# Stick-breaking attention: value product by query tiles on the two halves of the array, issued for two steps together

## The chip, the cores and the metric

The kernel runs on one core of one Trainium2 chip. The metric is the device time of one execution in microseconds (us). Each number of the trace comes from one profiled execution. In the text, PE is TensorE, DVE is VectorE, ACT is ScalarE, POOL is GpSimd, SP is the engine that issues the transfers.

## The reference

One residual block over 2048 tokens of width 1024 in float32: an RMSNorm, one wide input projection, a state-space branch (SSD), a stick-breaking attention branch of 16 heads of size 64, gates, an output projection and a second RMSNorm. The change touches the attention branch alone, cut here to what matters:

```python
def stick_breaking(q, k, v):
    for blk in range(L // SB_BLOCK):                       # 128 queries
        logits = einsum('bqhd,bkhd->bhqk', q[:, q0:kend], k[:, :kend]) * scale
        mask = ki < qi
        log_fail = where(mask, log_sigmoid(-logits), 0.0)
        between = cumsum(log_fail, axis=3, reverse=True) - log_fail
        w = where(mask, exp(log_sigmoid(logits) + between), 0.0)
        outs.append(einsum('bhqk,bkhd->bqhd', w, v[:, :kend]))
...
y_sb = einsum('ble,ed->bld', o * silu(z_sb), w_sb_proj)
```

## The kernel before

Products that need full precision (the projections, `proj` in the trace) are written as three products of rounded float32 pieces: high by high, high by low, low by high (`product`, L139). Each is a matmul of 128 rows, 128 columns and 512 moving columns. All matmuls and transposes are chained in program order (`chain`, L68), so the order on PE is the order in the code. The other engines' orders are set by a planner from the program, the priorities and the buffers.

The attention works on **steps** `(h, qs, kc)` (L778): a head, a block of 512 queries, a block of 512 keys with `kc <= qs`, taken from the diagonal `kc == qs` down to 0. A head has ten steps: four on the diagonal, six off it; there are 160 steps. A step has four query tiles `i` of 128 queries:

- `attn_qk(s, i)` (L826): two matmuls give the logits `lg` (PSUM, two buffers); ACT makes two sigmoids, `tc` (L840) and `sw` (L842). POOL masks both on the diagonal; DVE runs the product scan over `tc` (L849) and multiplies it into `sw` (L850). POOL keeps the carry for the next key block (L853).
- `attn_tr(s, i)` (L859): PE transposes the 128x128 pieces of `sw` into `wtp` (PSUM, three buffers), ACT copies them to `wt` (L870), which collects the weights of the whole step, keys on partitions, for the four key pieces `kb`.
- `attn_av(s)` (L872): the value product. For each of the four `kb`, the stationary operand is `v[:, kb, :]` (128 keys by 64 columns) and the moving one `wt[:, kb, :]`. Even `kb` write partitions 0 to 63 of `po`, odd `kb` 64 to 127, so that two of them can run on the two halves of the array's columns. On the diagonal, `kb` 2 and 3 leave out the queries ahead of them, `kb` 1 doesn't: POOL sets that corner of `wt` to zero (L869).
- After the last step of a query block (`kc == 0`): ACT copies one half of `po` (L889), DVE adds the other (L890) and multiplies by the gate `zl` (L891), which a transfer brought (L887). The result leaves to `otd` (L892).

The step loop (L902 to L910) runs `attn_tr(s, i)`, then `attn_qk(s + 1, i)`, then `fill(i)`: some projection matmuls that are not part of the attention, given out evenly over the steps (`fill`, L787; 24 of them make one tile of a projection). After `i == 1` comes `attn_av(s - 1)` and one more filling, `fill(CPB)`. In the last head the filling comes from the next stage (`fill_y`, L765), which needs a norm across tokens first (`first_y`, L737). Then follow the output projections (from L917), which read `otd`.

Of the kernel before, what the change touches and what calls it, by code (L numbers as in the profile page):

```python
# [9 lines left out]
F32 = mybir.dt.float32  # L10
# [8 lines left out]
P = 128  # L19
D = 1024  # L20
KT = D // P
TB = 512
HEADS = 16
HD = 64
# [24 lines left out]
def hybrid_kernel(ctx, tc, x, norm_pre, w_in, b_gate, conv_w, conv_b, dt_bias, a_log, d_skip,  # L49
                  ssd_norm, w_ssd_proj, w_sb_proj, w_out, norm_post, out, dbg=None):  # L50
    nc = tc.nc
# [3 lines left out]
    CPB = TB // P  # L55
# [12 lines left out]
    def chain(i):  # L68
        if last_pe[0] is not None:
            after(i, last_pe[0])  # L70
        last_pe[0] = i

    def matmul(*a, **k):
        chain(nc.tensor.matmul(*a, **k))  # L74

    def transpose(*a):
        chain(nc.tensor.transpose(*a))  # L77

    def opened(*a, **k):
        cm = tc.tile_pool(*a, **k)  # L80
        return cm.__enter__(), lambda: cm.__exit__(None, None, None)
# [31 lines left out]
    otd = [drp.tile([D, TB], F32, name=f"otd{t}") for t in range(NTB)]  # L113
    zsd = [drp.tile([D, TB], F32, name=f"zsd{t}") for t in range(NTB)]
# [94 lines left out]
    gz, close_gz = opened(name="gz", bufs=2)  # L209
# [433 lines left out]
    ab, close_ab = opened(name="ab", bufs=1)  # L643
    ap, close_ap = opened(name="ap", bufs=1, space=PSUM)
# [120 lines left out]
    def fill_y(box):  # L765
        tb, mp, y = TBO[0], box["mp"], box["y"]
        for dt in range(KT):
            w = prep_w(wa, WA, w_ssd, dt * P)
            ps = pp.tile([P, TB], F32, name="proj", tag="pp")
            yield from product(ps, w, *y)  # L770
            gt = piece("o")
            nc.sync.dma_start(gt, gtd[tb][dt * P:(dt + 1) * P, :])
            nc.vector.tensor_mul(mp[:, dt, :], gt, ps)
# [4 lines left out]
    steps = [(h, qs, kc) for h in range(HEADS) for qs in reversed(range(NTB)) for kc in reversed(range(qs + 1))]  # L778
# [3 lines left out]
    def tick():  # L782
        clock[0] += 1
        while events and events[0][0] <= clock[0]:
            heapq.heappop(events)[2]()

    def fill(i):  # L787
        f = fills
        if f["pos"] <= 0:
            for _ in f["gen"]:  # L790
                tick()
            if f["late"]:
                return
            f.update(gen=fill_y(box_y), left=8 * 24, pos=len(FW) * (len(steps) - last_head) - 3, acc=0.0, late=True)
        f["acc"] += f["left"] / f["pos"] * FW[i]
        f["pos"] -= 1
        while f["acc"] >= 1.0:
            f["acc"] -= 1.0
            f["left"] -= 1
            if next(f["gen"], 0) == 0:  # L800
                f["left"] = 0
                break
            tick()

    kts, vts, qts, pos, carry, ws = {}, {}, {}, {}, {}, {}

    def attn_load(s):
        if s >= len(steps):
            return
        h, qs, kc = steps[s]  # L810
        if (h, qs) not in qts:
            qa = ab.tile([P, TB], F32R, name="qa", tag="qa", bufs=2)
            qb = ab.tile([P, TB], F32R, name="qb", tag="qb", bufs=2)
            cols = slice(qs * TB, (qs + 1) * TB)
            nc.sync.dma_start(qa.bitcast(F32), qst[h][:, cols])
            nc.sync.dma_start(qb[0:HD].bitcast(F32), qst[h][HD:P, cols])
            nc.sync.dma_start(qb[HD:P].bitcast(F32), qst[h][0:HD, cols])
            qts[h, qs] = qa, qb
        if (h, kc) not in kts:
            k = ab.tile([P, TB], F32R, name="kt", tag="kt", bufs=4)  # L820
            nc.sync.dma_start(k.bitcast(F32), kst[h][:, kc * TB:(kc + 1) * TB])
            v = ab.tile([P, CPB, HD], F32, name="vt", tag="vt", bufs=4)
            nc.sync.dma_start(v, vst[h // 4][:, h % 4, kc * CPB:(kc + 1) * CPB, :])
            kts[h, kc], vts[h, kc] = k, v

    def attn_qk(s, i):  # L826
        if s >= len(steps):
            return
        h, qs, kc = steps[s]
        diag = kc == qs  # L830
        W = (i + 1) * P if diag else TB
        qa, qb = qts[h, qs]
        k = kts[h, kc]
        qc = slice(i * P, (i + 1) * P)
        lg = ap.tile([P, TB], F32, name="lg", tag="lg", bufs=2)
        matmul(lg[:, :W], qa[:, qc], k[:, :W], start=True, stop=False)
        matmul(lg[:, :W], qb[:, qc], k[:, :W], start=False, stop=True)
        t = ab.tile([P, TB + 1], F32, name="tc", tag="tc", bufs=5)
        nc.gpsimd.memset(t[:, W:W + 1], 1.0)  # L839
        nc.scalar.activation(t[:, :W], lg[:, :W], AF.Sigmoid, scale=-0.125)  # L840
        w = ab.tile([P, TB], F32, name="sw", tag="sw", bufs=6)
        nc.scalar.activation(w[:, :W], lg[:, :W], AF.Sigmoid, scale=0.125)  # L842
        if diag:
            nc.gpsimd.affine_select(out=t[:, W - P:W], in_=t[:, W - P:W], compare_op=ALU.is_gt, fill=1.0, base=0,  # L844
                                    pattern=[[-1, P]], channel_multiplier=1)
            nc.gpsimd.affine_select(out=w[:, W - P:W], in_=w[:, W - P:W], compare_op=ALU.is_gt, fill=0.0, base=0,
                                    pattern=[[-1, P]], channel_multiplier=1)
        tr = t[:, W::-1]
        nc.vector.tensor_tensor_scan(tr, tr, tr, 1.0 if diag else carry[h, qs, i], ALU.mult, ALU.min)  # L849
        nc.vector.tensor_mul(w[:, :W], w[:, :W], t[:, 1:W + 1])  # L850
        if kc > 0:
            c = ab.tile([P, 1], F32, name="cy", tag="cy", bufs=8)
            nc.gpsimd.tensor_copy(c, t[:, 0:1])  # L853
            carry[h, qs, i] = c
        ws[s, i] = w

    wts = {}

    def attn_tr(s, i):  # L859
        h, qs, kc = steps[s]  # L860
        n = i + 1 if kc == qs else CPB
        tp = ap.tile([P, TB], F32, name="wtp", tag="wtp", bufs=3)
        sw = ws.pop((s, i))
        for kb in range(n):
            transpose(tp[:, kb * P:(kb + 1) * P], sw[:, kb * P:(kb + 1) * P], ident)
        if i == 0:
            wts[s] = ab.tile([P, CPB, TB], F32, name="wt", tag="wt", bufs=2)
            if kc == qs:
                nc.gpsimd.memset(wts[s][:, 1, 0:P], 0.0)  # L869
        nc.scalar.copy(wts[s][:, 0:n, i * P:(i + 1) * P], tp[:, 0:n * P].rearrange("p (k q) -> p k q", q=P))  # L870

    def attn_av(s):  # L872
        h, qs, kc = steps[s]
        if (h, qs) not in pos:
            pos[h, qs] = ap.tile([P, TB], F32, name="po", tag="po", bufs=1)
        po, v = pos[h, qs], vts[h, kc]
        wt = wts.pop(s)
        for kb in range(CPB):
            lo = kb * P if kc == qs and kb > 1 else 0
            e = (kb % 2) * HD  # L880
            matmul(po[e:e + HD, lo:], v[:, kb, :], wt[:, kb, lo:], start=(kc == qs and kb < 2),
                   stop=(kc == 0 and kb >= 2), skip_group_check=True)
        if kc == 0:
            e0 = (h % 2) * HD
            mine, other = slice(e0, e0 + HD), slice(HD - e0, P - e0)
            z = ab.tile([P, TB], F32, name="zl", tag="zl", bufs=1)
            nc.sync.dma_start(z[mine], zsd[qs][h * HD:(h + 1) * HD, :])  # L887
            o = gz.tile([P, TB], F32, name="o", tag="gz", bufs=2)
            nc.scalar.copy(o[mine], po[other])  # L889
            nc.vector.tensor_add(o[mine], o[mine], po[mine])  # L890
            nc.vector.tensor_mul(o[mine], o[mine], z[mine])  # L891
            nc.sync.dma_start(otd[qs][h * HD:(h + 1) * HD, :], o[mine])  # L892

    attn_load(0)
    attn_load(1)
    for tb in range(NTB):
        if tb == NTB - 1:
            for i in range(CPB):
                later(1 + 6 * i, lambda i=i: attn_qk(0, i))
        run(proj(wg, tb, done_g(0, tb)))  # L900
    flush()
    for s in range(len(steps)):  # L902
        attn_load(s + 2)
        for i in range(CPB):
            attn_tr(s, i)
            attn_qk(s + 1, i)
            fill(i)
            if i == 1 and s > 0:
                attn_av(s - 1)
                fill(CPB)  # L910
    attn_av(len(steps) - 1)
    for _ in fills["gen"]:
        pass
# [3 lines left out]
    with tc.tile_pool(name="fc", bufs=1) as fc, tc.tile_pool(name="fp", bufs=1, space=PSUM) as fp:  # L917
# [65 lines left out]
        for it, tb in enumerate(TBO):  # L983
# [3 lines left out]
            for dt in range(KT):  # L987
# [11 lines left out]
                po = pp.tile([P, TB], F32, name="proj", tag="pp")  # L999
# [65 lines left out]
```

## Time and profile before

| | us |
|---|---|
| time, median of 3 runs (lowest to highest) | 3057.37 (3057.05 to 3060.44) |
| time of the profiled execution | 3057.36 |
| its span, first to last instruction | 3055.6 |
| PE busy | 3012.0 (99%) |
| DVE busy | 2140.1 (70%) |
| ACT busy | 1585.5 (52%) |
| POOL busy | 505.3 (17%) |
| value product: busy PE, in 1280 records | 283.5 |
| copy of one half of the product on ACT, 64 times, median of one | 0.58 |

The value products stand between 943 and 2556 us of the span. A float32 matmul of the value product is two records in the trace; a transpose and a matmul of rounded float32 are one. Ends of matmuls are modelled and overlap with the next, so the times between the starts tell how fast PE goes, not the durations.

### The profile page before, as it was taken

The numbers are of one execution on the slowest core, as the hardware profiler recorded it, in microseconds if no ns is written. First come the engines' busy times: TensorE is split into PE (matmuls) and PEld (weight loads), VectorE is DVE, ScalarE is ACT, GpSimd is POOL, SyncE is SP. The second block draws the span as 40 slices with busy tenths as digits, with TensorE's granted clock in tenths as the row PEclk, the third lists the DMA queues.
The fourth block names the chain that finished last, engine by engine and source line by source line (L and its number), as shares of the span: only waits on it lengthen the run. The fifth ranks groups of instructions, "written<-read, shape, count | busy, mean of one in ns | idle before, by whom it ended". The sixth has DMA issues, their size and how long they took to land.

```text
span 3055.6 us, 47953 instructions
## 1 busy us (share of the span) xinstructions
PE 3012.0 (99%) x16169; PEld 2342.6 (77%) x16169; DVE 2140.1 (70%) x3653; ACT 1585.5 (52%) x3102; POOL 505.3 (17%) x1690
## 2 busy tenths in 40 slices
PE   8999999999999999999999999999999999999998
PEld 6899888788887777777777777777777667888887
DVE  7310578868877777878778878877777798756653
ACT  6221345534546666666666666666666565333321
POOL 0000001001101222222222221222122331101000
PEclk9999999999999999999999999999999999999999
DMA  5522122202233333324323333334233345545452
GB/s 166 142 72 52 28 58 77 78 25 76 81 90 109 101 86 94 93 85 108 94 77 101 97 86 96 89 90 118 66 87 92 114 136 158 178 131 179 131 165 70
DMA packets 298812, 303.84 MB, mean 99 GB/s; under 512 B 55916, under 2 KB 196040, under 8 KB 298568
## 3 DMA queue, kind: packets, MB, share of 16 engines
q1 hardware_dynamic: 298416, 300.73, 34.3%
q8 instruction: 130, 2.13, 0.3%
q14 instruction: 114, 0.93, 0.1%
q10 hardware_dynamic: 152, 0.05, 0.0%
HBM read 208.28 MB, written 92.41 MB: 98 GB/s over the span
## 4 chain that ended last, share of the span: by engine, by line
PE 88%; DVE 7%; DMA 3%; issue 1%; ACT 0%; POOL 0%; SPq 0%; ACTq 0%; DVEq 0%; POOLq 0%
PE proj L74 49%; PE po L74 14%; PE lg L74 8%; PE wtp L77 8%; PE vps L74 6%; DMA csb<-csd 3%; DVE acc L472 1%; PE yp L74 1%; DVE S L538 1%; DVE csb L520 1%; DVE dl L518 1%; DVE dl L514 1%; PE stp L74 0%; DMA xt<-in_x 0%; DVE wlo L134 0%
## 5 line engine op out<-in xcount | busy, mean ns | idle before, releaser
L74 PE MATMUL proj<-hh,whi 128*128 128x512 f32 x1920 | 765.1, 398 | 0.0
L74 PE MATMUL proj<-hl,whi 128*128 128x512 f32 x1920 | 763.0, 397 | 1.1 <-DVE hl L286 0.9
L74 PE MATMUL proj<-hh,wlo 128*128 128x512 f32 x1920 | 763.8, 398 | 0.0
L870 ACT COPY wt<-wtp 128x512 f32<-128x512 f32 (+3 forms) x640 | 336.4, 526 | 396.2 <-PE wtp L77 374.5
L849 DVE TENSOR_TENSOR_SCAN tc<-tc,cy 128x513 f32<-128x513 f32 x384 | 491.7, 1281 | 56.0 <-ACT tc L840 52.3
L850 DVE TENSOR_TENSOR sw<-sw,tc 128x512 f32<-128x512 f32 (+3 forms) x640 | 400.8, 626 | 74.6 <-POOL cy L853 1.4
L74 PEld LDWEIGHTS proj<-hh,whi 128*128 128x128 f32 x1920 | 361.9, 188 | 102.2 <-issue 31.8
L74 PEld LDWEIGHTS proj<-hl,whi 128*128 128x128 f32 x1920 | 361.7, 188 | 102.0 <-issue 31.1
L74 PEld LDWEIGHTS proj<-hh,wlo 128*128 128x128 f32 x1920 | 361.5, 188 | 100.0 <-issue 31.1
L849 DVE TENSOR_TENSOR_SCAN tc<-tc 128x129 f32<-128x129 f32 (+3 forms) x256 | 220.6, 862 | 201.2 <-POOL tc L844 200.3
L840 ACT ACTIVATE tc<-lg 128x512 f32<-128x512 f32 (+3 forms) x640 | 346.3, 541 | 14.5 <-PE lg L74 3.2
L842 ACT ACTIVATE sw<-lg 128x512 f32<-128x512 f32 (+3 forms) x640 | 344.8, 539 | 0.0
L77 PE MATMUL wtp<-ident,sw 128*128 128x128 f32 x2176 | 341.7, 272 | 0.0
L77 PEld LDWEIGHTS wtp<-ident,sw 128*128 128x128 f32 x2176 | 275.5, 140 | 80.1 <-issue 0.3
L74 PE MATMUL lg<-kt,qa 128*128 128x512 f32 (+3 forms) x640 | 284.2, 444 | 2.7 <-ACT sw L842 2.5
L74 PE MATMUL po<-wt,vt 128*64 128x512 f32 (+2 forms) x1280 | 283.5, 554 | 1.7 <-ACT wt L870 1.7
L132 ACT CAST whi<-wraw 128x512 fp32r<-128x512 f32 x248 | 154.4, 623 | 240.9 <-PE proj L74 155.2
L74 PE MATMUL lg<-kt,qb 128*128 128x512 f32 (+3 forms) x640 | 234.3, 366 | 0.0
L134 DVE TENSOR_TENSOR wlo<-wraw,whi 128x512 fp32r<-128x512 f32 x246 | 174.2, 709 | 72.7 <-ACT whi L132 70.1
L74 PEld LDWEIGHTS po<-wt,vt 128*64 128x64 f32 x1280 | 77.9, 136 | 151.9 <-issue 139.1
L504 POOL TENSOR_TENSOR xe<-xd,dec 128x512 f32<-128x512 f32 x32 | 49.8, 1556 | 829.5 <-DVE xd L502 829.5
L839 POOL MEMSET tc<- 128x1 f32 x640 | 62.6, 98 | 739.5 <-DVE sw L850 720.0
(199 smaller groups left out, 4660.1 us busy)
## 6 DMA issues: line engine op xcount, KB each, us to landing
wraw<-in_w_in SPq DMA_DIRECT2D x120, 256.0 KB, 3.0
csb<-csd SPq DMA_DIRECT2D x64, 256.0 KB, 4.3
qa<-qst SPq DMA_DIRECT2D x64, 256.0 KB, 3.7
qb<-qst SPq DMA_DIRECT2D x128, 128.0 KB, 3.8
kt<-kst SPq DMA_DIRECT2D x64, 256.0 KB, 3.3
gtd<-zb SPq DMA_DIRECT2D x64, 256.0 KB, 2.1
wraw<-in_w_ssd_proj SPq DMA_DIRECT2D x64, 256.0 KB, 3.0
scr<-gtd SPq DMA_DIRECT2D x64, 256.0 KB, 3.2
```

The source lines that it names most:

```text
L74: chain(nc.tensor.matmul(*a, **k))
L77: chain(nc.tensor.transpose(*a))
L132: nc.scalar.copy(h, raw)
L134: (eng or nc.vector).tensor_tensor(l, raw, h.bitcast(F32), op=ALU.subtract)
L472: nc.vector.scalar_tensor_tensor(acc, xp[:, i:i + TB], pv[:, col:col + 1], acc, op0=ALU.mult, op1=ALU.add)
L504: nc.gpsimd.tensor_tensor(heads(xe), heads(xd), tok(dec), op=ALU.mult)
L839: nc.gpsimd.memset(t[:, W:W + 1], 1.0)
L840: nc.scalar.activation(t[:, :W], lg[:, :W], AF.Sigmoid, scale=-0.125)
L842: nc.scalar.activation(w[:, :W], lg[:, :W], AF.Sigmoid, scale=0.125)
L849: nc.vector.tensor_tensor_scan(tr, tr, tr, 1.0 if diag else carry[h, qs, i], ALU.mult, ALU.min)
L850: nc.vector.tensor_mul(w[:, :W], w[:, :W], t[:, 1:W + 1])
L870: nc.scalar.copy(wts[s][:, 0:n, i * P:(i + 1) * P], tp[:, 0:n * P].rearrange("p (k q) -> p k q", q=P))
```

## The change

`attn_av` gives each half of the array two of the four query tiles instead of two of the four key pieces. Tiles 0 and 3 go to partitions 0 to 63, tiles 1 and 2 to partitions 64 to 127 (`GROUPS`). So each `kb` is issued twice, with the same stationary operand, over 256 moving columns; for tiles 0 and 3 they lie in two runs of 128. On the diagonal, tiles that lie ahead of the key piece are left out one by one, and the zeroed corner isn't needed. All of a query's sum then lies in one half: the copy on ACT and the addition on DVE go, and one DVE product of 128x256 with the gate takes their place. The gate comes in two transfers instead of one, the result leaves in two.

The value products of steps `s - 2` and `s - 1` are issued together, at even `s`, after `i == 1`; those of the last two steps follow the loop. `fill(CPB)` keeps its place in every step, and stands in step 0 too. Buffers: `wt` 2 to 3, `po` 1 to 2 (of half the size), `zl` 1 to 2 (half), `wtp` 3 to 2, `tc` 5 to 4, `sw` 6 to 5.

```diff
-        t = ab.tile([P, TB + 1], F32, name="tc", tag="tc", bufs=5)
+        t = ab.tile([P, TB + 1], F32, name="tc", tag="tc", bufs=4)
...
-        w = ab.tile([P, TB], F32, name="sw", tag="sw", bufs=6)
+        w = ab.tile([P, TB], F32, name="sw", tag="sw", bufs=5)
...
-        tp = ap.tile([P, TB], F32, name="wtp", tag="wtp", bufs=3)
+        tp = ap.tile([P, TB], F32, name="wtp", tag="wtp", bufs=2)
...
-            wts[s] = ab.tile([P, CPB, TB], F32, name="wt", tag="wt", bufs=2)
-            if kc == qs:
-                nc.gpsimd.memset(wts[s][:, 1, 0:P], 0.0)
+            wts[s] = ab.tile([P, CPB, TB], F32, name="wt", tag="wt", bufs=3)
...
+    GROUPS = ((0, 3), (1, 2))
...
-            pos[h, qs] = ap.tile([P, TB], F32, name="po", tag="po", bufs=1)
+            pos[h, qs] = ap.tile([P, 2, P], F32, name="po", tag="po", bufs=2)
...
         for kb in range(CPB):
-            lo = kb * P if kc == qs and kb > 1 else 0
-            e = (kb % 2) * HD
-            matmul(po[e:e + HD, lo:], v[:, kb, :], wt[:, kb, lo:], start=(kc == qs and kb < 2),
-                   stop=(kc == 0 and kb >= 2), skip_group_check=True)
+            for g, (q0, q1) in enumerate(GROUPS):
+                ts = [t for t in (q0, q1) if kc < qs or t >= kb]
+                if not ts:
+                    continue
+                j0 = (q0, q1).index(ts[0])
+                step = (q1 - q0) * P
+                src = wt[:, kb, ts[0] * P:ts[0] * P + P]
+                if len(ts) == 2:
+                    src = wt[:, kb, :].rearrange("p (t q) -> p t q", q=P)[:, q0:q1 + 1:q1 - q0, :]
+                    dst = po[g * HD:(g + 1) * HD, :, :]
+                else:
+                    dst = po[g * HD:(g + 1) * HD, j0, :]
+                matmul(dst, v[:, kb, :], src, start=(kc == qs and kb == 0),
+                       stop=(kc == 0 and kb == (CPB - 1 if kc < qs else ts[-1])), skip_group_check=True)
         if kc == 0:
...
-            nc.sync.dma_start(z[mine], zsd[qs][h * HD:(h + 1) * HD, :])
-            o = gz.tile([P, TB], F32, name="o", tag="gz", bufs=2)
-            nc.scalar.copy(o[mine], po[other])
-            nc.vector.tensor_add(o[mine], o[mine], po[mine])
-            nc.vector.tensor_mul(o[mine], o[mine], z[mine])
-            nc.sync.dma_start(otd[qs][h * HD:(h + 1) * HD, :], o[mine])
+            zr = zsd[qs][h * HD:(h + 1) * HD, :].rearrange("d (t q) -> d t q", q=P)
+            orow = otd[qs][h * HD:(h + 1) * HD, :].rearrange("d (t q) -> d t q", q=P)
+            z = ab.tile([P, 2, P], F32, name="zl", tag="zl", bufs=2)
+            for g, (q0, q1) in enumerate(GROUPS):
+                nc.sync.dma_start(z[g * HD:(g + 1) * HD], zr[:, q0:q1 + 1:q1 - q0, :])
+            nc.vector.tensor_mul(z, z, po)
+            for g, (q0, q1) in enumerate(GROUPS):
+                nc.sync.dma_start(orow[:, q0:q1 + 1:q1 - q0, :], z[g * HD:(g + 1) * HD])
...
-            if i == 1 and s > 0:
+            if i == 1 and s > 0 and s % 2 == 0:
+                attn_av(s - 2)
                 attn_av(s - 1)
+            if i == 1:
                 fill(CPB)
+    attn_av(len(steps) - 2)
     attn_av(len(steps) - 1)
```

On PE, before, at the value product of the first step, which lies on the diagonal (`hh` and `hl` are the projections' moving operands, `whi` and `wlo` their weights):

```order
L74 MATMUL proj<-hh_195,wlo 128x512
L74 MATMUL po<-wt,vt 64x512 x2
L74 MATMUL po<-wt,vt 64x256
L74 MATMUL po<-wt,vt 64x128
L74 MATMUL proj<-hh_195,whi 128x512
```

and one step further down, at the value product of the second step, off the diagonal:

```order
L74 MATMUL proj<-hh_195,wlo 128x512
L74 MATMUL proj<-hh_196,whi 128x512
L74 MATMUL po<-wt,vt 64x512 x4
L74 MATMUL proj<-hl_200,whi 128x512
L74 MATMUL proj<-hh_196,wlo 128x512
```

On PE now, at the value products of the same two steps:

```order
L74 MATMUL proj<-hh_196,whi 128x512
L74 MATMUL po<-wt,vt 64x256 x2
L74 MATMUL po<-wt,vt 64x128
L74 MATMUL po<-wt,vt 64x256
L74 MATMUL po<-wt,vt 64x128 x3
L74 MATMUL po<-wt,vt 64x256 x8
L74 MATMUL proj<-hl_200,whi 128x512
L74 MATMUL proj<-hh_196,wlo 128x512
```

The two groups of value products have become one, with projection matmuls ahead of it and behind it as before; 4 and 4 matmuls have become 7 and 8, none of more than 256 columns.

On DVE, before, at the end of the third query block of the first head (L849 is the scan, L850 the product with it):

```order
L849 SCALAR_TENSOR_TENSOR tc<-tc 128x257
L850 TENSOR_TENSOR sw<-sw,tc 128x256
L890 TENSOR_TENSOR o<-o,po 64x512
L891 TENSOR_TENSOR o<-o,zl 64x512
L849 SCALAR_TENSOR_TENSOR tc<-tc 128x385
L850 TENSOR_TENSOR sw<-sw,tc 128x384
```

and now, at the end of its third and fourth query block:

```order
L849 SCALAR_TENSOR_TENSOR tc<-tc,cy 128x513
L850 TENSOR_TENSOR sw<-sw,tc 128x512
L899 TENSOR_TENSOR zl<-zl,po 128x256 x2
L849 SCALAR_TENSOR_TENSOR tc<-tc,cy 128x513
L850 TENSOR_TENSOR sw<-sw,tc 128x512
```

Two instructions per query block have become one; where a pair of steps ends two query blocks, both stand together, one step later for the first.

## Rows read from the trace of the kernel before

**Rows 1.** The page's busy time, share and instructions of an engine.
```profile
PE 3012.0 (99%) x16169; PEld 2342.6 (77%) x16169; DVE 2140.1 (70%) x3653; ACT 1585.5 (52%) x3102; POOL 505.3 (17%) x1690
```
**Rows 2.** Stretches: length, busy of PE, PEld, DVE, ACT, POOL; clock, DMA, GB/s.
```profile
930.00:1330.00 400.00, 400.00 (x2047) 286.56 (x2046) 316.19 (x393) 260.08 (x549) 98.37 (x402) 1.00 0.35 93
...
2410.00:2510.00 100.00, 91.27 (x449) 64.36 (x448) 84.64 (x122) 64.16 (x133) 38.03 (x93) 0.93 0.45 141
2510.00:2556.00 46.00, 41.63 (x212) 28.12 (x210) 39.96 (x52) 28.96 (x64) 14.53 (x36) 1.00 0.31 91
```
**Rows 3.** Timeline, start and length: value product off the diagonal, PE and PEld.
```profile
1706.87 0.40 PE L74 MATMUL proj<-hh,whi 128*128 128x512 f32 x1
...
1707.20 1.94 PE L74 MATMUL po<-wt,vt 128*64 128x512 f32 x8
1707.68 0.14 PEld L74 LDWEIGHTS po<-wt,vt 128*64 128x64 f32 x2 [0.29 <-issue]
...
1708.11 0.14 PEld L74 LDWEIGHTS po<-wt,vt 128*64 128x64 f32 x2 [0.28 <-issue]
...
1709.07 0.50 PE L74 MATMUL proj<-hl,whi 128*128 128x512 f32 x1
...
1709.40 0.39 PE L74 MATMUL proj<-hh,wlo 128*128 128x512 f32 x1
```
**Rows 4.** Instructions of that block by 1708.05: ns min/median/max, first and last start.
```profile
L74 PE MATMUL po<-wt,vt x4: 592/618/643, 1707.2 to 1707.7; 128*64 128x512 f32 x4
```
**Rows 5.** Timeline, start and length: value product on the diagonal.
```profile
1143.15 0.39 PE L74 MATMUL proj<-hl,whi 128*128 128x512 f32 x1
...
1143.38 0.40 PE L74 MATMUL proj<-hh,wlo 128*128 128x512 f32 x1
...
1143.70 1.50 PE L74 MATMUL po<-wt,vt 128*64 128x512 f32 x8
...
1145.14 0.50 PE L74 MATMUL proj<-hh,whi 128*128 128x512 f32 x1
...
1145.47 0.40 PE L74 MATMUL proj<-hl,whi 128*128 128x512 f32 x1
```
**Rows 6.** Half-array matmuls of 128 columns (SSD), 700.0 to 701.8, as rows 4.
```profile
L74 PE MATMUL yp<-dl,xd x16: 272/273/323, 700.1 to 701.5; 128*64 128x128 f32 x16
L74 PEld LDWEIGHTS yp<-csb,S x16: 137/137/137, 700.2 to 701.6; 128*64 128x64 f32 x16
L74 PE MATMUL yp<-csb,S x16: 272/273/273, 700.3 to 701.7; 128*64 128x128 f32 x16
```
**Rows 7.** The page's group of value products: busy us, mean ns | idle before.
```profile
L74 PE MATMUL po<-wt,vt 128*64 128x512 f32 (+2 forms) x1280 | 283.5, 554 | 1.7 <-ACT wt L870 1.7
```
**Rows 8.** Timeline of one step: a tile's way from logits to transposes; copies of `wtp`.
```profile
1701.72 0.60 PE L77 MATMUL wtp<-ident,sw 128*128 128x128 f32 x4
...
1702.35 0.59 ACT L870 COPY wt<-wtp 128x512 f32<-128x512 f32 x1 [0.57 <-PE wtp L77]
...
1705.26 0.38 PE L77 MATMUL wtp<-ident,sw 128*128 128x128 f32 x2
...
1705.40 0.48 PE L74 MATMUL lg<-kt,qa 128*128 128x512 f32 x1
...
1709.40 0.69 DVE L850 TENSOR_TENSOR sw<-sw,tc 128x512 f32<-128x512 f32 x1
...
1715.48 0.60 PE L77 MATMUL wtp<-ident,sw 128*128 128x128 f32 x4
```
**Rows 9.** The same timeline: an issue on SP.
```profile
1712.69 0.59 SPq L887 DMA_DIRECT2D zl<-zsd  x1
```
**Rows 10.** Waits of SP, 940 to 2560: total, times, longest.
```profile
SPq L892 <- DVE o L891: 180.7, 60, 8.2
```
**Rows 11.** Waits of PE, 2410 to 2556, the two longest, columns as rows 10.
```profile
PE sps L74 <- DVE scr L708: 3.9, 1, 3.9
PE proj L74 <- ACT zb L203: 3.6, 1, 3.6
```

More of the change, by code (lines that the diff above doesn't have):

```diff
@@ L878, in attn_av @@
         for kb in range(CPB):
-            lo = kb * P if kc == qs and kb > 1 else 0
-            e = (kb % 2) * HD
-            matmul(po[e:e + HD, lo:], v[:, kb, :], wt[:, kb, lo:], start=(kc == qs and kb < 2),
-                   stop=(kc == 0 and kb >= 2), skip_group_check=True)
-        if kc == 0:
-            e0 = (h % 2) * HD
-            mine, other = slice(e0, e0 + HD), slice(HD - e0, P - e0)
-            z = ab.tile([P, TB], F32, name="zl", tag="zl", bufs=1)
-            nc.sync.dma_start(z[mine], zsd[qs][h * HD:(h + 1) * HD, :])
-            o = gz.tile([P, TB], F32, name="o", tag="gz", bufs=2)
-            nc.scalar.copy(o[mine], po[other])
-            nc.vector.tensor_add(o[mine], o[mine], po[mine])
-            nc.vector.tensor_mul(o[mine], o[mine], z[mine])
-            nc.sync.dma_start(otd[qs][h * HD:(h + 1) * HD, :], o[mine])
+            for g, (q0, q1) in enumerate(GROUPS):
[12 more added lines that the diff above has]
+                       stop=(kc == 0 and kb == (CPB - 1 if kc < qs else ts[-1])), skip_group_check=True)
+        if kc == 0:
+            zr = zsd[qs][h * HD:(h + 1) * HD, :].rearrange("d (t q) -> d t q", q=P)
[6 more added lines that the diff above has]
+                nc.sync.dma_start(orow[:, q0:q1 + 1:q1 - q0, :], z[g * HD:(g + 1) * HD])
     attn_load(0)
```

## Prediction

> **What bounds the kernel now.** I read the page's busy table first. PE is busy for 3012.0 of 3055.6 us, every other engine far less [rows 1]. Then the table of stretches, because a mean hides stages. In the attention PE is busy for the whole 400 us of the stretch, DVE for 316 and ACT for 260 [rows 2]; PE has no wait of any length there. So in 15 heads a microsecond of PE's time is a microsecond of the kernel's. The last head differs: PE is idle for some 13 us of 146, and its mean granted clock is 0.93 in one stretch of 100 us [rows 2]. The stretches up to 925 us and from 2556 us hold no code that the change touches.
>
> Busy PE is modelled, so I take what a value product costs from the times between starts, in the timeline of one step, on both kinds of step.
>
> **A value product now.** Off the diagonal, the projection matmul ahead starts at 1706.87, the product at 1707.20, the projection matmuls behind at 1709.07 and 1709.40 [rows 3]: 2.53 us for the product and two intervals between projection matmuls. Such an interval is 0.23 (1143.15 to 1143.38 [rows 5]), so the product costs 2.53 - 0.46 = **2.07**. Its eight records go in pairs, one on each half: the weight loads show the pairs 0.43 apart (1707.68, 1708.11 [rows 3]). Four pairs are 4 x 0.43 = 1.72; the remaining **0.35** is paid at the edges: the pause until the first weights go in, the first record's longer stay (643 ns against 592 [rows 4]), and the same again on the way back.
>
> On the diagonal the times are 1143.38, 1143.70, 1145.14, 1145.47 [rows 5]: 2.09 - 0.46 = **1.63**. Here one half has two records of 512 columns and two of 256, 0.43 + 0.43 + 0.215 + 0.215 = 1.29, the other less; the edges are 0.34, as above.
>
> **The edges.** Two products issued together have nothing between them that uses the full array. The order shows one group of `po` matmuls with projections ahead and behind. 160 groups become 80, so 80 x 0.35 = **28.0 us** leave PE. Nothing hides the edges now, as PE is full there.
>
> **The columns.** Off the diagonal each half streams 8 records of 256 columns. No row of before has a long run of 256; it has 512 at 0.43, so 0.215 each in proportion, and a run of 128-column records on the halves in the SSD stage: 32 in 16 pairs from 700.1 to 701.7 [rows 6], 0.11 a pair, so at most 0.22 for 256. I take 0.216, nearer to 512 since the 128s themselves are almost in proportion (0.43 / 4 = 0.108): 1.73 against 1.72, a loss of 96 x 0.01 = 1 us; at 0.22 it would be 4 us. On the diagonal tiles 0 and 3 have, over four `kb`, 256 + 3 x 128 columns, tiles 1 and 2 have 2 x 256 + 128: 640 columns on either half, two records each, 2 x 0.216 + 6 x 0.11 = 1.09 against 1.29. 64 diagonal steps x 0.20 = **12.8 us**. A group is over when its fuller half is, and the new split is even.
>
> **The weights twice.** Each `v` piece now goes to both halves: 8 loads more off the diagonal, 6 more on it, 1152 records more than the 1280 of [rows 7]. In [rows 6] a load takes 137 ns from start to end, and there is one for every 128-column matmul, two per 0.11 us: they run beside the matmuls. So I take nothing for them; if that cover were gone, each record would pay about 0.05 as the first does [rows 4].
>
> "TensorE: Matmul & The Clock Gate" of the Trainium skill ("The mechanism") says against this change that a weight load overlaps with matmuls in flight only where the row groups differ; here all loads take all 128 rows. [Rows 6] don't agree: the loads there take all rows as well. By that rule the time would be that of the second rival below. "TensorEngine Tiling" of the Trainium skill ("Instruction Overhead") gives about 60 cycles for every matmul: an estimate of 25 ns x 1152, over two halves 14 us, which would make 3032. [Rows 6] show some 2 ns beyond the proportion.
>
> **The other engines.** ACT loses a copy per query block and DVE one of two instructions; neither sets the pace, so I count nothing. POOL loses 64 settings of a corner. SP gets one more gate load and one more result write per query block, 128 issues of some 0.6 [rows 9], 77 us over 1600. What is queued behind a result write on SP (loads of `kt`, `qa`, `vt`, weights) waits with it for DVE, 180.7 us in all before [rows 10], without any wait of PE on a transfer. Where a pair ends two query blocks, the first product on DVE comes one step later, and one SP write with it; the loads behind are for a step or a weight tile ahead. I count nothing; if a load came late, PE would pay its landing, some 3 us, once.
>
> **The buffers.** PE's queue holds the transposes of a tile one step behind its logits. A tile with logits at 1705.40 has its last DVE product from 1709.40 to 1710.09, and its transposes start at 1715.48 [rows 8]: 5.4 us to spare. The group of value products grows from 2.07 to at most 2 x 1.73 + 0.35 = 3.8, so DVE, which waits for it with the scans queued behind, can hold a tile back by 1.7 more. Two `wtp` buffers mean that transposes wait for the copy of the tile but one before: the copy of 1702.35 ends at 1702.94, the transposes that would need it start at 1705.26 [rows 8], 2.3 to spare. `tc` with four buffers waits for the product of the same tile a step earlier, and PE has by then transposed that very tile. No cost.
>
> **The sum.** A head has 6 steps off the diagonal and 4 on it. Before: 6 x 2.07 + 4 x 1.63 = 18.94. After: 6 x 1.73 + 4 x 1.09 + 5 x 0.35 = 16.49. 2.45 us a head, **39.2 us** in 16 heads, which is the 28.0 and 12.8 less the 1, to the rounding. The profiled execution took 3057.36 us, its span 3055.6 and 1.8 around it, and is the median of the runs. 3057.4 - 39.2 = **3018**.
>
> What is unknown within this: the last head. Two waits of 3.9 and 3.6 us there come from the norm of the next stage [rows 11], the low clock (0.93 of 100 us is some 14 us at the lower of the two levels, 1.2 instead of 2.4 GHz) follows such waits, and PE comes to them elsewhere in its order now. The head's own 2.45 can be lost in them, or one wait with its low clock (3.9 + 3.5) come or go: 3010 to 3026. With 256 columns at 0.22 it is 3021.
>
> **Rivals.**
>
> *One: half of it is not there.* Edges inside a joined group stay, because PE stops at the second product for its own buffer or its weights' copy: then only the columns gain, 12.8 - 1, and the time is 3046; with part of them 3026 to 3046. For it: the second product waits on other semaphores than the first. Against it: `po` has two buffers, and `wt` was copied some 4 us before. Chance 0.08.
>
> *Two, slower: short records with their weights in the open.* If a half can't load the next weights of the same length of matmul beside it, every record pays: 8 on the fuller half in each of 160 steps. At 0.05 each that is 64 us, and the time is 3082. It decides from 39.2 / (160 x 8) = 0.031 us a record. For it: the first record pays that, and every `v` piece is read twice. Against it: [rows 6], 2 ns. Between, at 0.01 to 0.03, it is 3031 to 3056. Chance of slower 0.03, of between 0.05.
>
> *Three, slower: the tiles arrive late.* DVE needs 316 us of 400 [rows 2], and and a step without a value product gives it little more than it needs: a step lasts 10.1 us (943 to 2556 over 159 steps), 10.1 - 2.07 = 8.1 of PE against 0.79 x 10.1 = 8.0 of DVE. If PE then waited 0.5 us behind each of the 80 groups, the gain would be gone; at 1 us it would be 3098. Against it: 5.4 us to spare, DVE loses work, and over two steps it has 20.2 us as before less 0.5. Chance 0.03.
>
> *Four: more than forecast.* The waits in the last head go, with their clock: 3018 less 8 to 13, 3005 to 3010. Chance 0.06.
>
> **How the numbers follow.** The forecast, 3018 with 3010 to 3026, has 0.75. The range reaches over rival four's nearer part and the 14 us of a fixed cost per record or a part of rival one: 3007 to 3035, with about 0.83 in it. About 0.2%, 6 us, is what a measurement of this kernel can tell from no change. Faster by more: the forecast, rival four, most of one and of the between case, 0.92. Within 0.2%: the far ends of those, 0.02. Slower: rivals two and three, 0.06.
>
> **What would show it.** In the profile after: 80 groups of `po` records on PE, a diagonal and an off-diagonal product together in about 3.2 us from the projection ahead to the one behind less two intervals, two off the diagonal in 3.8; the pairs of 256-column records 0.216 apart; PE busy over the whole of its stretches in the first 15 heads; the last value product some 39 us earlier, near 2516. Wrong would be: pairs over 0.24 apart, a pause inside a group, PE waiting for `sw`, `wtp` or a transfer between 930 and 2370, or more of the low clock in the last head.

## The result, and the profile after

The changed kernel takes **3018.37 us** (median, 3016.26 to 3019.43) against 3057.21 before: the ratio is 0.9868, 95% interval 0.9854 to 0.9883, so 38.8 us less by the medians. The forecast was 3018. The profiled execution took 3019.43 us, its span is 3017.7.

The page's busy time and its group of value products, which answer to [rows 1] and [rows 7]:

```profile
PE 2973.3 (99%) x17321; PEld 2436.5 (81%) x17321; DVE 2078.2 (69%) x3589; ACT 1551.7 (51%) x3038; POOL 473.9 (16%) x1626
...
L74 PE MATMUL po<-wt,vt 128*64 128x256 f32 (+1 forms) x2432 | 253.6, 361 | 0.0
```

PE lost 38.7 us of busy time, and is as full as before. The value product has 2432 records instead of 1280, 1152 more, and 30 us less of busy time. DVE, ACT and POOL are lighter too, which, as the experiments show, is worth nothing here.

The timeline of a group of two products off the diagonal, and of one on and one off it, answers to [rows 3] and [rows 5]:

```profile
1368.08 0.39 PE L74 MATMUL proj<-hh,wlo 128*128 128x512 f32 x1
...
1368.39 3.67 PE L74 MATMUL po<-wt,vt 128*64 128x256 f32 x32
1372.00 0.50 PE L74 MATMUL proj<-hh,whi 128*128 128x512 f32 x1
1372.34 0.40 PE L74 MATMUL proj<-hl,whi 128*128 128x512 f32 x1
```

```profile
1348.68 0.39 PE L74 MATMUL proj<-hh,whi 128*128 128x512 f32 x1
...
1348.99 3.03 PE L74 MATMUL po<-wt,vt 128*64 128x256 f32 x30
1351.95 0.50 PE L74 MATMUL proj<-hl,whi 128*128 128x512 f32 x1
1352.29 0.39 PE L74 MATMUL proj<-hh,wlo 128*128 128x512 f32 x1
```

Read as before the change, less two intervals of 0.23: 4.26 - 0.46 = 3.80 for two products off the diagonal, where two groups took 2 x 2.07 = 4.14; and 3.61 - 0.46 = 3.15 for a mixed pair, where they took 1.63 + 2.07 = 3.70. The same group's instructions one by one (count, ns min/median/max, first and last start):

```profile
L74 PEld LDWEIGHTS po<-wt,vt x32: 132/137/137, 1368.4 to 1371.5; 128*64 128x64 f32 x32
L74 PE MATMUL po<-wt,vt x32: 379/379/430, 1368.4 to 1371.7; 128*64 128x256 f32 x32
```

32 records are 16 pairs, and from the first to the last start it is 3.3 us or 15 intervals: 0.22 each. Only one pair shows the longer 430 ns of a first load; all other loads lie beside matmuls, and there is no pause where the second product begins.

The stretches of the attention, columns as [rows 2]:

```profile
930.00:1330.00 400.00, 400.00 (x2375) 317.54 (x2376) 309.08 (x388) 260.89 (x552) 93.37 (x401) 1.00 0.35 97
...
2370.00:2470.00 100.00, 91.14 (x524) 70.46 (x521) 82.48 (x120) 64.14 (x136) 43.03 (x96) 0.97 0.48 147
2470.00:2518.00 48.00, 43.94 (x270) 33.50 (x271) 40.35 (x52) 30.83 (x68) 14.30 (x37) 1.00 0.35 99
```

PE is full up to 2370 us, that is in 14 heads and most of the 15th, with no wait on `sw`, `wtp` or a transfer. From there on it is idle for 12.9 of 148 us, against 13.1 of 146 before [rows 2].

How much a head gained is read from the first transposes of the second and of the 15th head, in the timelines of before and of after:

```profile
1029.72 0.27 PE L77 MATMUL wtp<-ident,sw 128*128 128x128 f32 x1
...
2335.69 0.27 PE L77 MATMUL wtp<-ident,sw 128*128 128x128 f32 x1
```

```profile
1031.87 0.27 PE L77 MATMUL wtp<-ident,sw 128*128 128x128 f32 x1
...
2303.98 0.27 PE L77 MATMUL wtp<-ident,sw 128*128 128x128 f32 x1
```

1305.97 us for 13 heads have become 1272.11: **2.60 a head**, where 2.45 was forecast. The second head begins 2.15 later, though one head's gain lies ahead of it: some 5 us were lost earlier, in code that the change doesn't touch. Two stretches there, of before and then of after, show with what:

```profile
30.00:70.00 40.00, 36.44 (x206) 28.93 (x206) 32.51 (x89) 24.39 (x41) 0.00 (x0) 1.00 0.38 121
600.00:640.00 40.00, 34.31 (x203) 28.22 (x203) 31.42 (x77) 21.58 (x30) 3.57 (x1) 0.96 0.19 53
```

```profile
30.00:70.00 40.00, 35.52 (x183) 27.84 (x181) 30.19 (x85) 22.59 (x38) 0.00 (x0) 0.91 0.34 115
600.00:640.00 40.00, 34.52 (x199) 28.26 (x198) 32.23 (x79) 19.34 (x29) 3.57 (x1) 0.91 0.22 61
```

The granted clock was lower in both (0.91 against 1.00 and 0.96): a part of each stretch ran at the lower of the two levels, 1.2 instead of 2.4 GHz, in the first one soon after waits of PE for DVE of 1.4 and 1.7 us. 0.09 and 0.05 of 40 us are 5.6 us at the full clock, about what was lost. In the first stretch this is not the change: another profiled execution of the same kernel (`changed_again`, below) has 1.00 there with much the same waits (4.1 us in all against 4.5), reaches the attention 6.6 us earlier (930.64 against 937.25) and has a span of 3011.6. In the second it has 0.91 as well, so that a part of the change in that is not ruled out. A single execution of one kernel may thus differ from another by 6 us through what happens ahead of the attention.

### The profile page after: what moved, and what is told of

Read it like the earlier page. It is cut to its first block, busy times and chain, and to the rows that moved or that the text cites. A ratio compares the mean times of both kernels' runs of the same rounds, so it can differ in the third digit from the quotient of the medians.

```text
span 3017.7 us, 50157 instructions
## 1 busy us (share of the span) xinstructions
PE 2973.3 (99%) x17321; PEld 2436.5 (81%) x17321; DVE 2078.2 (69%) x3589; ACT 1551.7 (51%) x3038; POOL 473.9 (16%) x1626
## 4 chain that ended last, share of the span: by engine, by line
PE 88%; DVE 7%; DMA 3%; ACT 1%; issue 1%; POOL 0%; SPq 0%; DVEq 0%; ACTq 0%; POOLq 0%
PE proj L74 49%; PE po L74 14%; PE lg L74 8%; PE wtp L77 8%; PE vps L74 6%; DMA csb<-csd 2%; DVE acc L472 1%; PE yp L74 1%; DVE S L538 1%; DVE dl L514 1%; DVE csb L520 1%; DVE dl L518 1%; PE stp L74 1%; DVE wlo L134 0%; PE xtp L77 0%
## 5 line engine op out<-in xcount | busy, mean ns | idle before, releaser
L849 DVE TENSOR_TENSOR_SCAN tc<-tc,cy 128x513 f32<-128x513 f32 x384 | 494.7, 1288 | 82.3 <-ACT tc L840 77.5
L850 DVE TENSOR_TENSOR sw<-sw,tc 128x512 f32<-128x512 f32 (+3 forms) x640 | 399.4, 624 | 76.7 <-ACT tc L840 0.5
L849 DVE TENSOR_TENSOR_SCAN tc<-tc 128x129 f32<-128x129 f32 (+3 forms) x256 | 222.4, 869 | 190.0 <-POOL tc L844 189.7
L74 PE MATMUL po<-wt,vt 128*64 128x256 f32 (+1 forms) x2432 | 253.6, 361 | 0.0
L74 PEld LDWEIGHTS po<-wt,vt 128*64 128x64 f32 x2432 | 164.8, 137 | 88.0 <-issue 29.6
```

## The experiments

All times are medians, each with the ratio to the kernel before on the same chip and its 95% interval. For the changed kernel the ratio was 0.9868 in the first comparison.

**One half of the change, and the other.** `tiles_only` keeps the product by query tiles and issues it in every step:

```diff
-            if i == 1 and s > 0 and s % 2 == 0:
-                attn_av(s - 2)
+            if i == 1 and s > 0:
                 attn_av(s - 1)
```

> The value product by query tiles alone: one group in every step, as before, with the buffers of the changed kernel. Theory (edges and columns are separate terms): the 80 edges are back, the columns' gain stays: 64 x 0.20 - 96 x 0.01 = 11.8 us less than before, 3045; the trace shows 160 groups, about 1.42 us from the first record to the projection behind on the diagonal less the edge, 1.09 + 0.35 in all, and 1.73 + 0.35 off it. Rival (the gain is the work taken from ACT, DVE and POOL, or the shorter epilogue): the time stays near the changed kernel's, 3018 to 3025.

Measured: 3047.17 us, ratio 0.9964 (0.9952 to 0.9977), 11.0 us less than before (3058.15 there). The timeline of a product on the diagonal:

```profile
943.70 0.40 PE L74 MATMUL proj<-hh,wlo 128*128 128x512 f32 x1
944.03 1.30 PE L74 MATMUL po<-wt,vt 128*64 128x256 f32 x14
945.26 0.50 PE L74 MATMUL proj<-hh,whi 128*128 128x512 f32 x1
945.60 0.40 PE L74 MATMUL proj<-hl,whi 128*128 128x512 f32 x1
```

1.90 - 0.46 = 1.44, as expected (1.09 + 0.35). This kernel has the short epilogue, so ACT, DVE and POOL have the changed kernel's lighter work: the rival, that this makes the gain, falls.

`pairs_only` is the other half: the product by key pieces with its copy and addition, two steps together.

```diff
+            if i == 1 and s > 0 and s % 2 == 0:
+                attn_av(s - 2)
+                attn_av(s - 1)
...
             matmul(po[e:e + HD, lo:], v[:, kb, :], wt[:, kb, lo:], start=(kc == qs and kb < 2),
                    stop=(kc == 0 and kb >= 2), skip_group_check=True)
```

> The value products of two steps together, but each by key pieces as before, with the copy, the addition and the corner set to zero as before (po and zl two buffers of full size, sw four). Theory: 80 edges of 0.35 go, 28.0 us less than before, 3029; a pair off the diagonal takes 2 x 1.72 + 0.35 = 3.8. Rival (an edge is also paid inside a group, when the second product starts with its own weights and its own semaphore): 14 us or less, 3043 to 3057. Second rival (old columns leave a hole between the products, since one half ends 0.2 earlier on the diagonal and the next product fills it): up to 64 x 0.2 / 2 more gain, 3023.

Measured: 3031.39 us, ratio 0.9914 (0.99 to 0.9929), 26.8 us less than before. Two products off the diagonal:

```profile
971.64 0.40 PE L74 MATMUL proj<-hl,whi 128*128 128x512 f32 x1
971.97 3.65 PE L74 MATMUL po<-wt,vt 128*64 128x512 f32 x16
975.55 0.50 PE L74 MATMUL proj<-hh,wlo 128*128 128x512 f32 x1
975.89 0.39 PE L74 MATMUL proj<-hh,whi 128*128 128x512 f32 x1
```

4.25 - 0.46 = 3.79: a second product adds its columns and no edge. The first rival (an edge inside a group) falls; so does the second, since the time is 3031, not 3023. 26.8 + 11.0 = 37.8 of 38.8, each with some 4 us of uncertainty: the halves add up, as terms of one engine's time do.

**Do short records cost?** `records_halved` issues each 256-column matmul as two of 128:

```diff
-                matmul(dst, v[:, kb, :], src, start=(kc == qs and kb == 0),
-                       stop=(kc == 0 and kb == (CPB - 1 if kc < qs else ts[-1])), skip_group_check=True)
+                for t in ts:
+                    matmul(po[g * HD:(g + 1) * HD, (q0, q1).index(t), :], v[:, kb, :], wt[:, kb, t * P:t * P + P],
+                           start=(kc == qs and kb == 0),
+                           stop=(kc == 0 and kb == (CPB - 1 if kc < qs else ts[-1])), skip_group_check=True)
```

> The changed kernel with each 256-column matmul of the value product as two of 128, with the same weights loaded for each. Theory (a short record costs 2 ns beyond its columns and weights load beside it): 96 x 16 x 0.001 + some, 3 us more than the changed kernel, 3021. Rival (weights of short records in the open, 0.05 each): 8 records more per half off the diagonal and 2 on it, 96 x 8 x 0.05 + 64 x 2 x 0.05 = 45 us more, 3063, slower than before.

Measured: 3023.15 us, ratio 0.9885 (0.987 to 0.99). In it the second `start` of a half set back the sum that the first had begun in other columns, so part of the value product is missing from its output, which is off by 0.11 (relative error). `records_one_start` has the same instructions with one start:

```diff
-                           start=(kc == qs and kb == 0),
+                           start=(kc == qs and kb == 0 and t == ts[0]),
```

> As records_halved, but of the two first matmuls of a half only the first begins a new sum (there the second began one as well, which set back the sum of the first, so its output wasn't the whole value product). The same instructions otherwise. Theory (a short record costs about 2 ns): as records_halved, 5 us more than the changed kernel, 3023. Rival (the time of records_halved came from the second start): back to 3018 or up.

Measured: 3023.18 us, ratio 0.9888 (0.9874 to 0.9903). A group of two products off the diagonal in it:

```profile
972.80 0.40 PE L74 MATMUL proj<-hl,whi 128*128 128x512 f32 x1
973.12 3.77 PE L74 MATMUL po<-wt,vt 128*64 128x128 f32 x64
976.82 0.50 PE L74 MATMUL proj<-hh,wlo 128*128 128x512 f32 x1
977.16 0.40 PE L74 MATMUL proj<-hh,whi 128*128 128x512 f32 x1
```

4.36 - 0.46 = 3.90 against 3.80 with half as many records: 16 more on each half cost 0.10 us, 6 ns each on average. (The longest but the first pair takes 317 ns instead of 273, and the other starts are 0.11 apart, so half of it is one late record.) That is not the 50 of weights in the open nor the 31 from which the change would have lost; it is three times the 2 ns that the forecast read from [rows 6]. By the medians the two kernels are 5 us (other chip) and 7 us (same chip) behind the changed one; their intervals overlap with its.

**Does the balance of the halves count?** `neighbours` gives tiles 0 and 1 to one half and 2 and 3 to the other:

```diff
-    GROUPS = ((0, 3), (1, 2))
+    GROUPS = ((0, 1), (2, 3))
```

> The changed kernel with tiles 0 and 1 on one half, 2 and 3 on the other. Both moving operands are one run. On the diagonal one half then has 384 columns, the other 896. Theory (the fuller half sets a diagonal product's length): 2 x (3 x 0.216 + 0.109) = 1.51 instead of 1.09, 64 x 0.42 = 27 us more than the changed kernel, 3045, if the emptier half can't run ahead into the next product; if it can, a pair that ends off the diagonal is no shorter either, as the fuller half stays the longer. Rival (two runs cost something in the moving operand): less than 27 more, by what the runs cost off the diagonal: at 0.01 a record 96 x 8 x 0.01 = 8 us, 3037.

Measured: 3037.91 us, ratio 0.9936 (0.9921 to 0.9951). A mixed pair in it:

```profile
953.17 0.40 PE L74 MATMUL proj<-hh,whi 128*128 128x512 f32 x1
953.50 3.46 PE L74 MATMUL po<-wt,vt 128*64 128x256 f32 x28
956.89 0.50 PE L74 MATMUL proj<-hl,whi 128*128 128x512 f32 x1
957.22 0.39 PE L74 MATMUL proj<-hh,wlo 128*128 128x512 f32 x1
```

4.05 - 0.46 = 3.59 against 3.15: 0.44 in each of 64 pairs, 28 us on PE. The fuller half sets the time, as expected. The kernel's time shows 21 us by the ratios, with some 6 of uncertainty, and the spans 19 and 25 (3036.7 against 3017.7 and 3011.6 of the changed kernel's two profiled executions); the length of a head, in the table below, shows 27. So the gain on the diagonal hangs on the pairing of a long tile with a short one: with neighbours, the diagonal products would be 14 us slower than those before (64 x (1.51 - 1.29)).

**Does the place count, and are there more edges to save?** Beside the changed kernel on the same chip:

> The changed kernel itself, beside the others of this call: 3018, as a measure of what two calls on the chip can differ by.

Measured: 3016.01 us, ratio 0.9866 (0.9851 to 0.988).

`pairs_at_end` issues the pairs at the end of every second step, with two `wt` buffers; `threes_at_end` up to three steps there, with three (its edit is shown; `pairs_at_end` has 2 in place of 3):

```diff
-            if i == 1 and s > 0 and s % 2 == 0:
-                attn_av(s - 2)
-                attn_av(s - 1)
             if i == 1:
                 fill(CPB)
+        held.append(s)
+        if len(held) == 3 or len({st[:2] for st in steps[held[0]:s + 2]}) > 2 or s == len(steps) - 1:
+            for d in held:
+                attn_av(d)
+            held.clear()
-    attn_av(len(steps) - 2)
-    attn_av(len(steps) - 1)
```

> The changed kernel with its pairs issued at the end of every second step, after the last filling, with two wt buffers. As many edges and columns as the changed kernel. Theory (only the number of edges and the columns count, not the place): 3018. Rival (the place costs: wait for the last copy of wt, transposes behind instead of a projection): 80 x 0.2 = 16 us more, 3034.

Measured: 3015.53 us, ratio 0.9865 (0.9848 to 0.9881). By the medians the place costs nothing, and the rival's 16 us are ruled out. Two `wt` buffers are enough up to 2350 us, where PE waits for nothing; after that its value products wait 4.6 us for ACT's copies into `wt`, which they don't in the changed kernel.

> The changed kernel with the value products of up to three steps together, issued at the end of a step after its last filling (so that three wt buffers do); a group stops at two query blocks, since po has two buffers. 56 groups instead of 80. Theory (0.35 an edge, PE the bound): 24 x 0.35 = 8.4 us less than the changed kernel, 3010. Rival (tiles arrive late behind a group of 3 x 1.73 + 0.35 = 5.5 us, or PE waits for the last copy of wt, which it now needs within one filling): 0.5 us of waits of PE on ACT or DVE in each of 56 groups eat it, 3038; the waits of PE between 930 and 2370 us would show it.

Measured: 3010.47 us, ratio 0.9846 (0.9831 to 0.9861): 5.5 us less than the changed kernel beside it, of 8.4 expected. PE waits for nothing between 930 and 2350 us; a group of three, one product on the diagonal and two off it, is this:

```profile
959.53 0.40 PE L74 MATMUL proj<-hl,whi 128*128 128x512 f32 x1
959.86 4.76 PE L74 MATMUL po<-wt,vt 128*64 128x256 f32 x46
964.55 0.66 PE L77 MATMUL wtp<-ident,sw 128*128 128x128 f32 x4
```

4.69 us from its first record to the transposes, with which the next step begins. What is missing shows at the end of the attention. The stretch there, of `threes_at_end` and then of `changed_again`:

```profile
2360.00:2510.00 150.00, 131.94 (x779) 103.55 (x778) 121.56 (x172) 93.61 (x201) 56.32 (x132) 0.97 0.44 130
```

```profile
2370.00:2520.00 150.00, 135.73 (x798) 104.16 (x797) 125.11 (x177) 93.62 (x200) 54.18 (x127) 0.99 0.44 132
```

PE is idle for 18.1 us of 150 against 14.3. The last run was to show whether the long groups cause that, with pairs as in the changed kernel in the last head alone:

```diff
+            if i == 1 and s > last_head and s % 2 == 0:
+                attn_av(s - 2)
+                attn_av(s - 1)
...
+        if s >= last_head:
+            continue
         held.append(s)
```

> threes_at_end once more, as it was, beside the next kernel on the same chip: 3010, with PE idle for 18 us from 2360 us on.

> threes_at_end up to the end of the 15th head, and the changed kernel's pairs (after the second tile of even steps) in the last one, where threes_at_end left PE idle for 18 us from 2360 us on and the changed kernel for 13. Theory (the longer groups at the end of a step are late only where the next stage's norm keeps ACT and POOL busy): 5 us less than threes_at_end, 3005, and PE idle for 13 us in the last head. Rival (the idle time there is the next stage's chain, whatever the groups): 3010, and 18 us idle, or the head's own edge gone as well, 3011.

Measured: 3013.20 us, ratio 0.9845 (0.9831 to 0.9858), and 3012.19 us, ratio 0.9838 (0.9825 to 0.9851), with 3060.15 before on this chip. The same stretch of the first and of the second:

```profile
2360.00:2516.00 156.00, 138.11 (x795) 108.18 (x794) 122.60 (x174) 95.87 (x204) 57.52 (x134) 0.95 0.44 127
```

```profile
2360.00:2516.00 156.00, 138.90 (x789) 106.05 (x788) 123.28 (x173) 93.13 (x201) 55.92 (x128) 0.96 0.43 125
```

17.9 and 17.1 us idle, and times that can't be told apart. But this run doesn't decide between theory and rival, because most of the extra idle time lies ahead of its edit. The longest wait of `threes_last_head_pairs`, for the sums of the next stage's norm (`sps`), and the first transposes of its last head:

```profile
2378.80 1.41 PE L74 MATMUL sps<-ones,mp 128*128 128x1 f32 x6 [3.94 <-POOL tc L839]
...
2402.48 0.33 PE L77 MATMUL wtp<-ident,sw 128*128 128x128 f32 x1
```

The wait stands in the 15th head, where this kernel still has groups of three. In both versions with threes it is 3.9 or 4.0 us, in `changed_again` 0.3, and from 2360 us to the last head PE is idle for 6.3 us in both, against 3.6. In the last head itself, idle times are 10.8 us with pairs, 11.6 with threes and 10.7 in `changed_again`. Why this wait is long behind groups of three, as it was before the change (3.9, [rows 11]), and short in the changed kernel, stays open. By the ratios, the runs with threes are 6 to 9 us faster than the changed kernel; most of the intervals overlap.

**What a head takes.** Times of one kernel differ by some us, but between the first transposes of the second and of the 15th head PE never waits, and there two executions of the changed kernel agree to 0.01 us. A head of each run, from the starts of these transposes (`threes_at_end`: to the 14th head, as its groups repeat every two heads):

| | from | to | us a head | less than before | less, as forecast |
|---|---|---|---|---|---|
| before | 1029.72 | 2335.69 | 100.46 | | |
| `tiles_only` | 1030.36 | 2326.17 | 99.68 | 0.78 | 4 x 0.20 - 6 x 0.01 = 0.74 |
| `pairs_only` | 1027.25 | 2308.96 | 98.59 | 1.87 | 5 x 0.35 = 1.75 |
| changed | 1031.87 | 2303.98 | 97.85 | 2.60 | 2.45 |
| `changed_again` | 1025.25 | 2297.37 | 97.86 | 2.60 | 2.45 |
| `records_one_start` | 1028.28 | 2306.21 | 98.30 | 2.16 | 2.45 - 5 / 16 = 2.14 |
| `neighbours` | 1028.84 | 2323.09 | 99.56 | 0.90 | 2.45 - 4 x 0.42 = 0.77 |
| `pairs_at_end` | 1030.04 | 2298.50 | 97.57 | 2.88 | 2.45 |
| `threes_at_end` | 1030.30 | 2195.59 | 97.11 | 3.35 | 2.45 + 8.4 / 16 = 2.98 |

The two halves, 0.78 and 1.87, make 2.65 of 2.60. `neighbours` takes 1.70 more than the changed kernel, 27 us in 16 heads, as expected. Short records cost 0.45, 7 us in 16 heads. At the end of a step the pairs are 0.28 cheaper, 4.5 us in 16 heads, less than the medians can show; no run tells why. Of the 0.75 that threes gain on the changed kernel, 0.47 is left beside the pairs in the same place, for 3.5 groups a head instead of 5: 0.31 an edge.

## Why the prediction was right

**The edges.** Forecast 28.0 us for 80 of them. `pairs_only` took away the edges alone and measured 26.8, and 1.87 a head, 29.9 in 16. An edge, read once more from the pairs, is 4.14 - 3.79 = 0.35.

**The columns.** Forecast 12.8 less 1. `tiles_only` measured 11.0, and 0.78 a head, 12.5 in 16; its diagonal product has the expected length to 0.01 us. `neighbours` shows that the balance, not the smaller number of columns alone, makes it.

**The weights twice.** Taken at nothing, from [rows 6]. `records_one_start` doubles nearly all records and loads and pays 6 ns for each on average. The rule that loads overlap only between different row groups ("TensorE: Matmul & The Clock Gate" of the Trainium skill, "The mechanism") doesn't hold for the two column halves here: 32 loads of all rows within 3.3 us, 137 ns each, and the matmuls don't wait. The 60 cycles a matmul of "TensorEngine Tiling" of the Trainium skill ("Instruction Overhead") don't show either: a further matmul, of two records, costs 12 ns in `records_one_start`, and 60 cycles are an estimated 25 ns. The forecast had put these 25 on each of 1152 records, which are 576 matmuls: by the Trainium skill's figure the estimate would have been 7 us, not 14.

**The other engines.** Taken at nothing. `pairs_only` keeps the copy, the addition and the corner, and has its whole gain; `tiles_only` drops them and has no more than the columns. Behind the longer groups no tile came late before 2350 us, even with three products together.

**What the forecast missed.** A head gained 2.60, not 2.45, on PE; the groups themselves account for 2.07 x 6 + 1.63 x 4 - 3.80 - 4 x 3.15 = 2.54. What the forecast calls the last head begins earlier: before the change, too, the longer of its two waits is in the 15th.

```profile
2429.00 1.27 PE L74 MATMUL sps<-ones,mp 128*128 128x1 f32 x6 [3.89 <-DVE scr L708]
...
2448.52 0.27 PE L77 MATMUL wtp<-ident,sw 128*128 128x128 f32 x1
```

The second line is the first transpose of the 16th head. The buffers were taken at no cost, and behind 2370 us PE now waits for `wtp`. PE's waits after 2370 us (total, times, longest):

```profile
PE wtp L77 <- ACT wt L868: 6.0, 5, 2.0
PE wtp L77 <- DVE sw L850: 1.8, 1, 1.8
PE proj L74 <- ACT zb L203: 1.7, 1, 1.7
...
PE sps L74 <- DVE scr L708: 0.3, 1, 0.3
```

The two waits of [rows 11], 3.9 and 3.6, have become 0.3 and 1.7, but transposes now wait 6.0 us for ACT's copies, and 12.9 us idle stand against some 13 before: the idle time came out even by two changes that the forecast had only as a range. `tiles_only` and `pairs_only`, with two `wtp` buffers as well, wait 4.9 and 7.1 us there, the kernel before, with three, not at all; that the buffers are the cause fits this, but no run has the change with three. The clock fell less there: the mean of 100 us was 0.97, where it had been 0.93 [rows 2].

**What was luck.** That 3018.37 meets 3018 so closely. In the profiled executions the attention, from the first transposes to the projection behind the last value product, took 1624.31 us before (931.77 to 2556.08) and 1581.20 after (937.25 to 2518.45):

```profile
931.77 0.27 PE L77 MATMUL wtp<-ident,sw 128*128 128x128 f32 x1
...
2556.08 0.50 PE L74 MATMUL proj<-oh,whi 128*128 128x512 f32 x1
```

```profile
937.25 0.27 PE L77 MATMUL wtp<-ident,sw 128*128 128x128 f32 x1
...
2518.45 0.50 PE L74 MATMUL proj<-oh,whi 128*128 128x512 f32 x1
```

It gained 43.1 us where 39.2 were forecast, and the 5.5 lost ahead of it hid that. `changed_again` took 3016.01, 40.9 us less than before on its chip. The mechanism and its terms hold; a match to the microsecond is more than they can promise.

## What to carry to other kernels

Where TensorE is the bound, an instruction stream that changes between the full array and its column halves can pay at each change (here 0.35 us a visit), however good each part is: count the visits, and join them as far as buffers allow. With work on two halves, the fuller half is the time, so pair a long piece with a short one. And what is saved on engines that nobody waits for can be left out of the sum.

## What the runs showed of the hardware

A visit of value products to the column halves cost 0.35 us beside their columns (4.14 - 3.79), and nothing more between two products in one visit. The starts of float32 records on a half stood 0.43 us apart for 512 moving columns, 0.22 for 256, 0.11 for 128, and doubling the records cost 6 ns for each further one on average; 64 loads of 64 weight columns, 137 ns each, fitted beside 64 records of 128 columns, all within 3.77 us. Moving operands in two runs of 128 cost no more than one run of 256: with `neighbours`, where all are one run, two products off the diagonal take the same 3.80 us in each of the 16 groups of its trace. A `start` in one half set back a sum in other columns of the same half: `records_halved` lost part of its output (relative error 0.11), `records_one_start` didn't.
